# Output projection of a hybrid attention block as a Strassen product over pairs of token tiles

## Chip, cores, metric

One core of a Trainium2 chip runs the kernel. The metric is the device time of one execution in microseconds. Engines are named as in the profile: PE (TensorE), DVE (VectorE), ACT (ScalarE), POOL (GpSimd), SP (SyncE, which here only issues DMAs); PEld is PE's weight load.

## The reference

One layer over 1024 tokens of width 1024, all in float32. The lines around the change:

```python
h = rmsnorm(x, norm_mix_pre)
proj = h @ w_in                     # q, k, v, forget, conv parts, two gates
...                                 # short convolution ya, forgetting attention yb
merged = sigmoid(gate_conv) * (ya @ w_branch[0]) + sigmoid(gate_attn) * (yb @ w_branch[1])
m = merged @ w_out                  # 1024 x 1024 by 1024 x 1024
x = x + rmsnorm(m, norm_mix_post)
h = rmsnorm(x, norm_ffn_pre)
f = (silu(h @ w_gate) * (h @ w_up)) @ w_down
out = x + rmsnorm(f, norm_ffn_post)
```

The output is (1, 1024, 1024) in float32.

## The kernel before

*Precision.* Each float32 operand is split into a high part, `hi` = the value rounded to fp32r by an ACT copy, and a low part, `lo` = value minus `hi`, a DVE subtraction (`split`). A product is three matmuls: hi*hi, hi*lo, lo*hi (`mm3`). So each operand costs one ACT pass and one DVE pass, and all 128x128 by 128x512 matmuls come in threes.

*Strassen.* The projections and the FFN already use the Strassen-Winograd form on 2x2 blocks: seven products (A11 B11, A12 B21, S1 T1, S2 T2, S3 T3, S4 B22, A22 T4) instead of eight. `prod` is one product of 12 matmuls (4 blocks along K, three each) into a PSUM bank; `strassen` runs the products and combines them with DVE additions (`c12`, `c22`, `c21`; P1 = A11 B11 is kept, c11 comes out of the bank `b1`). `prep_first` and `prep_rest` load a weight pair into `raw`, make the S sums on DVE (in the one buffer `sx` and in place) and split them. A product that adds to a bank must wait until DVE has read the bank's earlier content.

*Stages, in order.* (1) v projection. (2) 18 projection jobs (`jobs`: four q/k, four `z`, two `gb`, eight gates), the operands of two jobs prepared ahead. (3) Attention, with the conv branch's products as filler. (4) `pbb`: the attention branch's product by `w_branch[1]`, for two token halves `n` and eight column blocks `d`, gated by `sg` loads and added into `um`, which is [128, 8, 1024], the merged activations with the width on the partitions. While `n` is 0, one row block of `w_out` a step is loaded and split into `woh`/`wol`. (5) `e_mm`/`e_norm`: for each of eight 128-token tiles, 2 x 8 x 3 matmuls into two `pm` banks, then the post-norm, the residual sum, the store of the new `x` to `x2_dram`, the FFN's pre-norm, eight transposes (`tp`) and two copies back into `um`. The norm of a tile runs under the matmuls of the next. (6) `f_first` for seven FFN columns: only P1 and c11, which need only the first four tiles; they are stored in `pre_dram`. The last tile's norm runs under the first four. `h2_sums` makes, for four slices, the T operands of the FFN, slice `sl` out of tiles `sl` and 4+`sl`; each uses `sx` for T1 and T2 and a `raw` for T3 and T4. (7) The FFN columns and (8) the down projection.

*Order.* A scheduler of the language places each instruction on its engine's queue by its own model; the queues run in order. The lists in `strict` fix program order for some stages (attention); stages (4) to (7) have none. Buffers are `wpool` tiles: `raw` 3, `hi` 4, `lo` 3, `sx` 1, `s4` 1, `s4h`/`s4l` 2 each.

All arithmetic goes through small helpers, so the profile gives one line, L76, to nearly every instruction (the call in `InOrder`); groups are told apart by tile names. There `c` stands for c12, c21, c22, `b` for the banks b1 to b3, `s` for s4 and others, since numbers are left out.

Of the kernel before, what the change touches and what calls it, by code (L numbers as in the profile page):

```python
# [17 lines left out]
P = 128  # L18
# [28 lines left out]
def block_kernel(  # L47
# [69 lines left out]

    def copy(o, a):
        nc.scalar.activation(o, a, AF.Copy)
# [16 lines left out]
    stat.tile([P, 24], F32, name="pad", bufs=1)  # L136
# [12 lines left out]
    ri_dram = [dpool.tile([2, S], F32, name=f"ri_dram{j}") for j in range(4)]  # L149
    sg_dram = [dpool.tile([2, P, S], F32, name=f"sg_dram{d}") for d in range(8)]  # L150
# [195 lines left out]

    def v_tile(st, ops):
# [36 lines left out]
    for st in range(ST):  # L384
# [5 lines left out]
        if st + 3 == ST:  # L390
            ax_close()
            w0, w0_close = pool("w0", side="right")
            r0 = w0.tile([P, KT, P], F32, name="r0")
            h0, l0 = (w0.tile([P, KT, P], F32R, name=n) for n in ("h0", "l0"))
# [429 lines left out]

    zts = {}
# [3 lines left out]
    for ij, (kind, j, _, _) in enumerate(jobs):  # L829
# [57 lines left out]
        else:  # L887
# [286 lines left out]
    wo_pool, wo_close = pool("wo", side="right")  # L1174
    woh = wo_pool.tile([P, KT, D], F32R, name="woh")
    wol = wo_pool.tile([P, KT, D], F32R, name="wol")
# [25 lines left out]
    ha_pool, ha_close = pool("ha")  # L1202
    hah = ha_pool.tile([P, 2, 4, NC], F32R, name="hah")
    hal = ha_pool.tile([P, 2, 4, NC], F32R, name="hal")
    fp, fp_close = pool("f", 2)
    ep, ep_close = pool("e")
    gpo = bcast_row(norm_mix_post[0], ep, name="gpo")
    gpr = bcast_row(norm_ffn_pre[0], ep, name="gpr")

    def e_mm(st):  # L1210
        ss = slice(st * P, (st + 1) * P)
        mh, ml = hi_t(), lo_t()
        split(mh, ml, um[:, :, ss])
        pm = []
        for n in range(2):
            ns = slice(n * NC, (n + 1) * NC)
            ps = psm.tile([P, NC], F32, tag="mm", name="pm")
            for k in range(KT):
                mm3(
# [11 lines left out]
    def e_norm(st, pm):  # L1231
        ss = slice(st * P, (st + 1) * P)
        xt = xts.popleft()
        if st + 1 < ST:
            xts.append(load_xt(st + 1))
# [385 lines left out]
```

## Time and profile before

| | |
|---|---|
| median of 3 runs | 1350.15 us (1349.59 to 1350.45) |
| the profiled execution | 1350.04 us |
| its span, first to last instruction | 1348.2 us |
| PE busy | 1328.5 us (99%) |
| DVE busy | 932.3 us (69%) |
| ACT busy | 535.2 us (40%) |
| POOL busy | 127.2 us (9%) |
| `pm` matmuls, first to last start | 610.9 to 704.3 us |
| bytes moved by DMA | 186.36 MB |

Matmuls are pipelined and their ends are modelled: a busy PE says that work was queued. The spacing of starts says how fast it went. Idle time is shown before an instruction, with what released it. Timeline rows with a count merge neighbours of one kind.

### The profile page before, as it was taken

Reading aid. Unit: us, or ns where it says so; the run is one execution under the profiler, and the core shown is the slowest. Engines: PE = TensorE matmul, PEld = TensorE weight load, DVE = VectorE, ACT = ScalarE, POOL = GpSimd, SP = SyncE. Lnnn points to the kernel's source line nnn. Section 1 sums busy time; section 2 is a strip of 40 time slices with the busy share of each in tenths; the row PEclk is TensorE's granted clock in tenths of the full one; section 3 lists DMA queues with packets and bytes.
Section 4 is the critical chain, followed back from the end, with each engine's and each line's share of the span. In section 5 each row is a group of like instructions: output and inputs, shape, how many; then the busy total and the mean of one; then the engine's idle time right before and its main releaser. Section 6 shows DMA issues by size and latency. Waiting matters only on the chain.

```text
span 1348.2 us, 17709 instructions
## 1 busy us (share of the span) xinstructions
PE 1328.5 (99%) x6753; PEld 1098.9 (82%) x6753; DVE 932.3 (69%) x1445; ACT 535.2 (40%) x851; POOL 127.2 (9%) x252
## 2 busy tenths in 40 slices
PE   9999999999999999999999999999999999999997
PEld 7978888888887778788887788888888888888886
DVE  6974668754556766775669698776677766677585
ACT  6642222243345756613547232223222323444452
POOL 0001000011112112000002121100111011000000
PEclk9999999999999999999999999999999999999999
DMA  5332422333325444362235565332323236965541
GB/s 189 118 109 86 126 70 71 105 123 109 102 82 192 158 142 165 126 218 79 94 110 175 170 200 167 102 100 80 117 102 118 93 111 240 361 235 196 161 164 63
DMA packets 153256, 186.36 MB, mean 138 GB/s; under 512 B 9409, under 2 KB 106753, under 8 KB 153170
## 3 DMA queue, kind: packets, MB, share of 16 engines
q1 hardware_dynamic: 138434, 136.67, 32.4%
q0 software_dynamic: 14736, 48.54, 9.3%
q8 instruction: 53, 0.87, 0.3%
q14 instruction: 33, 0.27, 0.1%
HBM read 136.10 MB, written 49.09 MB: 137 GB/s over the span
## 4 chain that ended last, share of the span: by engine, by line
PE 58%; DVE 3%; DMA 2%; issue 1%; ACT 1%; POOL 0%; DVEq 0%; SPq 0%; POOLq 0%; ACTq 0%
PE b L76 28%; PE pd L76 15%; PE pm L76 5%; PE pbb L76 3%; PE pba L76 2%; PE po L76 1%; PE tps L76 1%; PE sp L76 1%; DMA pre_dram<-s 1%; DMA tk<-in_w_down_dram 1%; DVE tt L76 0%; DVE lo L76 0%; PE tp L76 0%; DMA pre_dram<-c 0%; ACT tt L76 0%
## 5 line engine op out<-in xcount | busy, mean ns | idle before, releaser
L76 DVE TENSOR_TENSOR c<-c,b 128x512 f32<-128x512 f32 x195 | 132.9, 682 | 91.4 <-PE b L76 72.3
L76 DVE TENSOR_TENSOR lo<-raw,hi 128x1024 fp32r<-128x1024 f32 (+1 forms) x93 | 112.0, 1204 | 83.1 <-PE b L76 68.8
L76 ACT ACTIVATE hi<-raw 128x1024 fp32r<-128x1024 f32 (+1 forms) x100 | 101.7, 1018 | 127.9 <-PE b L76 75.7
L76 PE MATMUL b<-hth,hi 128*128 128x512 f32 x352 | 137.3, 390 | 0.0
L76 PE MATMUL b<-hth,lo 128*128 128x512 f32 x352 | 137.0, 389 | 0.0
L76 PE MATMUL b<-htl,hi 128*128 128x512 f32 x352 | 136.9, 389 | 0.0
L76 ACT ACTIVATE hi<-sx 128x1024 fp32r<-128x1024 f32 x41 | 43.5, 1062 | 220.9 <-PE b L76 195.3
L76 PEld LDWEIGHTS b<-hth,hi 128*128 128x128 f32 x352 | 66.1, 188 | 14.6 <-DVE c L76 1.0
L76 PEld LDWEIGHTS b<-hth,lo 128*128 128x128 f32 x352 | 66.1, 188 | 13.8
L76 PEld LDWEIGHTS b<-htl,hi 128*128 128x128 f32 x352 | 66.1, 188 | 13.7
L76 DVE TENSOR_TENSOR lo<-sx,hi 128x1024 fp32r<-128x1024 f32 x41 | 50.2, 1224 | 33.6 <-PE b L76 31.4
L76 PE MATMUL b<-hah,hi 128*128 128x512 f32 x176 | 69.0, 394 | 1.2 <-ACT c L76 1.2
L76 PE MATMUL b<-hal,hi 128*128 128x512 f32 x176 | 68.5, 389 | 0.0
L76 PE MATMUL b<-hah,lo 128*128 128x512 f32 x176 | 68.4, 390 | 0.0
L76 DVE TENSOR_TENSOR sx<-raw 128x512 f32<-128x512 f32 x78 | 53.6, 688 | 19.1 <-DMA raw<-in_w_in_dram 9.0
L76 PE MATMUL pd<-hi,lo 128*128 128x512 f32 x160 | 62.3, 389 | 0.0
L76 PE MATMUL pd<-hi 128*128 128x512 f32 x160 | 62.0, 390 | 0.0
L76 PE MATMUL pd<-ghi 128*128 128x512 f32 x148 | 57.6, 390 | 0.0
L76 PE MATMUL pd<-glo,ghi 128*128 128x512 f32 x148 | 57.6, 389 | 0.0
L76 PE MATMUL pd<-ghi,glo 128*128 128x512 f32 x148 | 57.6, 389 | 0.0
L76 PE MATMUL b<-hT34h,hi 128*128 128x512 f32 x136 | 53.0, 390 | 0.4 <-DVE c L76 0.4
L76 PE MATMUL b<-hT34h,lo 128*128 128x512 f32 x136 | 52.9, 389 | 0.0
(368 smaller groups left out, 3359.9 us busy)
## 6 DMA issues: line engine op xcount, KB each, us to landing
raw<-in_w_gate_up_dram SPq DMA_DIRECT2D x51, 512.0 KB, 3.8
raw<-in_w_in_dram SPq DMA_DIRECT2D x35, 512.0 KB, 3.8
a_dramS<-um POOLq DMA_DIRECT2D x44, 256.0 KB, 2.8
a_dramA<-um POOLq DMA_DIRECT2D x33, 256.0 KB, 2.8
xt<-in_x_dram SPq DMA_DIRECT2D x16, 512.0 KB, 4.3
sg<-sg_dram SPq DMA_DIRECT2D x32, 256.0 KB, 4.6
graw<-a_dramS SPq DMA_DIRECT2D x14, 512.0 KB, 4.0
sg_dram<-c POOLq DMA_DIRECT2D x24, 256.0 KB, 2.3
```

The lines of the kernel that those rows point to most:

```text
L76: ins = getattr(self.engine, name)(*args, **kw)
```

## The change

`w_out` gets the Strassen form too, over pairs of 128-token tiles: A is the 2x2 of `um` (two halves of the width by two tiles of a pair), B is the 2x2 of `w_out`. Four pairs of seven products of 12 matmuls take the place of eight tiles of 48.

- *Weights.* `wo_ops(n)`, called once after each of 16 projection jobs, loads four 128x128 blocks of `w_out`, makes T1 to T4 with four POOL subtractions, splits all seven operands (896 wide) and stores the two parts in a new DRAM buffer `wo_dram`, [7, 4, 128, 2, 512], from POOL. `r0`, `h0`, `l0` have one buffer each.
- *`pbb`.* The loads and splits of `w_out` go; `load_wo` loads B11, B21, T2, T1 (16 x 512 KB, split already) between the `sg` loads. The operands of pair 0 and the sums of pairs 0 and 1 start in the second half.
- *Pairs.* `first`/`second` run A11 B11 and A12 B21 for all four pairs. The kept P1 and c11 of pairs 0 to 2 take the three `raw` buffers. Then, pair by pair, `rest_ops` of the next pair, the five other products, `e_norm` of the pair before. The S sums are POOL additions in place in `um` (`gtt`).
- *Norm.* `e_norm` now takes two tiles at once. POOL multiplies three of four blocks by the gain `gpo`, DVE adds to `x` in four half rows, and both tiles' transposes (16) follow. The scaled rows go into `tt` and into the kept buffer.
- *Buffers.* The `x` tiles of the weights become the FFN's operands afterwards (B11, B21 and T1 to T4 of the activations). While `f_first` runs, its P1 lies in halves of `sx`, not in an own buffer.

```diff
+    def wo_ops(n):
+        k, c = divmod(n, 4)
+        r, h, l = w0_tiles()
+        for slot, (row, half) in enumerate(((k, 1), (k, 0), (4 + k, 0), (4 + k, 1))):
+            nc.sync.dma_start(
+                r[:, slot], wout_d[row * P : (row + 1) * P, half * NC + c * P : half * NC + (c + 1) * P]
+            )
+        for o, a, b in ((4, 0, 1), (5, 3, 4), (6, 3, 0), (7, 2, 5)):
+            gtt(r[:, o], r[:, a], r[:, b], ALU.subtract)
+        split(h[:, 1:], l[:, 1:], r[:, 1:])
+        for hl, t in enumerate((h, l)):
+            nc.gpsimd.dma_start(
+                wo_dram[:, k, :, hl, c * P : (c + 1) * P].rearrange("o p m -> p o m"), f32(t[:, 1:])
+            )
...
+        if 0 < ij < len(jobs) - 1:
+            wo_ops(ij - 1)
...
+    def load_wo(o, k):
+        nc.sync.dma_start(f32(wo[o][:, :, k, :]), wo_dram[o, k])
...
             nc.sync.dma_start(sg, sg_dram[d][1, :, ns])
+            load_wo(*loads.pop(0))
...
-            if n == 0:
-                wr = flat(raw_t())
-                nc.sync.dma_start(wr, wout_d[d * P : (d + 1) * P, :])
-                split(woh[:, d, :], wol[:, d, :], wr)
+            if n and d == 1:
+                first_ops(0, [s4h_t(), s4h_t()], [s4l_t(), s4l_t()])
...
+    def first(i):
+        b1s[i] = bank(psm, "b1")
+        prod(b1s[i], firsts[i]["A11"], both(wo[B11]), True)
+        t = raw_t() if i < 3 else ep.tile([P, KT, P], F32, name="keep")
+        keeps.append(flat(t).rearrange("p (a b) -> p a b", a=2))
+        copy(keeps[i][:, 0], b1s[i])
+    def second(i):
+        b1 = b1s.pop(i)
+        prod(b1, firsts[i]["A12"], both(wo[B21]), False)
+        mul(keeps[i][:, 1], b1, gpo[:, n1])
+        square(b1, qas[i][:, 0:1])
...
+    def e_norm(i, c12, c21, c22):
+        qa, qb = qas[i], st2("qb")
+        for c, acc in ((c12, qb[:, 0:1]), (c21, qa[:, 1:2]), (c22, qb[:, 1:2])):
+            square(c, acc)
+        for c, ns in ((c12, n2), (c21, n1), (c22, n2)):
+            gtt(c, c, gpo[:, ns], ALU.mult)
+        add(qa, qa, qb)
+        rs = scale2(qa)
...
+        rs = scale2(ssq)
+        for e in range(2):
...
+            nc.vector.scalar_tensor_tensor(
+                tt[e], xp[e], rs[:, e : e + 1], gpr, op0=ALU.mult, op1=ALU.mult
+            )
...
+    for step in (0, 1, 2, 3):
+        first(step)
+        if step:
+            second(step - 1)
+    second(PAIRS - 1)
...
-    for st in range(ST):
-        cur = e_mm(st)
+    for i in range(PAIRS):
+        nxt = rest_ops(i + 1) if i + 1 < PAIRS else None
+        _, *cur = strassen(ops, wob, psm, fe, keeps[i][:, 0])
         if prev is not None:
-            e_norm(st - 1, prev)
...
+            e_norm(i - 1, *prev)
+        if i > 1:
+            half_split(B11, i - 2)
+        prev, ops = cur, nxt
+    hb.append(both(x_tile(2)))
+    for i in range(2):
+        half_split(B21, i)
+    p1s = flat(wtile("sx", 1))
     for f in range(4):
-        f_first(f)
-    e_norm(ST - 1, prev)
+        f_first(f, p1s[:, (n1, n2)[f % 2]])
+    e_norm(PAIRS - 1, *prev)
```

The order on the engines, at three places.

POOL during the projection jobs, before, where it only issues stores (`so` and `c` are results of the q/k jobs):

```order
L76 DMA qk_dram_67<-so 128x512
L76 DMA qk_dram_68<-so 128x512
L76 DMA qk_dram_67<-c_1128 128x512
L76 DMA qk_dram_67<-c_1114 128x512
L76 MEMSET s_1296 128x8
L76 DMA qk_dram_67<-c_1039 128x512
L76 DMA qk_dram_68<-c_1249 128x512
L76 DMA qk_dram_68<-c_1235 128x512
```

And after:

```order
L76 DMA qk_dram_67<-so 128x512
L76 TENSOR_TENSOR r_1297<-r_1297 128x128 x4
L76 DMA qk_dram_68<-so 128x512
L76 DMA wo_dram<-h_1298 128x7x128
L76 DMA wo_dram<-l_1299 128x7x128
L76 TENSOR_TENSOR r_1459<-r_1459 128x128 x4
L76 DMA wo_dram<-h_1460 128x7x128
L76 DMA qk_dram_67<-c_1129 128x512
L76 DMA wo_dram<-l_1461 128x7x128
L76 DMA qk_dram_67<-c_1115 128x512
L76 DMA qk_dram_67<-c_1040 128x512
```

The four subtractions and the two stores of each `wo_ops` call stand among the stores of the first jobs; the last of the 16 calls ends among the first four stores of `ya`, that is with the seventh job, not one for each job.

DVE where the norm of a late tile ends, before (tile 5; `tt` is what the transposes read, `lo<-raw,hi` the split of an FFN weight):

```order
L76 SCALAR_TENSOR_TENSOR tt<-pm,r_6379,gpo 128x512 x2
L76 TENSOR_TENSOR xt<-xt,tt 128x1024
L76 TENSOR_SCALAR va<-ssq 128x1
L76 RECIPROCAL r_6391<-sq 128x1
L76 SCALAR_TENSOR_TENSOR t_6395<-r_6391,va 128x1
L76 TENSOR_SCALAR t_6395<-t_6395 128x1
L76 TENSOR_TENSOR r_6396<-r_6391,t_6395 128x1
L76 SCALAR_TENSOR_TENSOR tt<-xt,r_6396,gpr 128x1024
L76 TENSOR_TENSOR lo<-raw,hi 128x1024
```

And after, where the norm of pair 2 ends (its two tiles are scaled into `tt` and `raw`; `keep` and `c_6560` belong to pair 3):

```order
L76 TENSOR_TENSOR c_6560<-c_6560,b_6547 128x512
L76 TENSOR_TENSOR lo<-raw,hi 128x1024
L76 TENSOR_SCALAR va<-ssq 128x2
L76 RECIPROCAL r_6650<-sq 128x2
L76 TENSOR_TENSOR t_6654<-r_6650,va 128x2
L76 TENSOR_TENSOR keep<-keep,b_6546 128x512
L76 TENSOR_TENSOR t_6654<-t_6654,r_6650 128x2
L76 TENSOR_TENSOR lo<-raw,hi 128x1024
L76 TENSOR_SCALAR t_6654<-t_6654 128x2
L76 TENSOR_TENSOR r_6655<-r_6650,t_6654 128x2
L76 SCALAR_TENSOR_TENSOR tt<-xt,r_6655,gpr 128x1024
L76 SCALAR_TENSOR_TENSOR raw<-xt,r_6655,gpr 128x1024
```

The split of the weight came behind the scaled rows and now two such splits come ahead of them, with the last sum of the next pair between; on PE the 16 transposes of the pair stand directly behind the 60 matmuls of the next pair.

DVE ahead of the first FFN product, before (`htl` and `hcl` are T and B22 operands of the activations, `sx` and `raw` their sums; the `sgf` row is the FFN's first gate):

```order
L76 SCALAR_TENSOR_TENSOR tt<-xt,r_6694,gpr 128x1024
L76 TENSOR_TENSOR htl<-sx,hth 128x8x128
L76 TENSOR_TENSOR htl<-raw,hth 128x8x128
L76 TENSOR_TENSOR lo<-raw,hi 128x1024
L76 TENSOR_TENSOR sx<-um 128x512
L76 TENSOR_TENSOR raw<-um 128x512
L76 TENSOR_TENSOR hcl<-um,hch 128x4x128 x3
L76 TENSOR_TENSOR sx<-um,sx 128x512
```

And after (`x_6923`, `x_6924`, `x_6925` and `x_6926` are T1, T2, T3 and T4):

```order
L76 SCALAR_TENSOR_TENSOR keep<-xt,r_6882,gpr 128x1024
L76 TENSOR_TENSOR lo<-raw,hi 128x1024
L76 TENSOR_TENSOR raw<-um 128x512
L76 TENSOR_TENSOR sgf<-sgf,c_7104 128x512
L76 TENSOR_TENSOR x_6925<-raw,x_6925 128x4x128
L76 TENSOR_TENSOR lo<-raw,hi 128x1024
L76 TENSOR_TENSOR sx<-um 128x512
L76 TENSOR_TENSOR sx<-um,sx 128x512
L76 TENSOR_TENSOR raw<-um,sx 128x512
L76 TENSOR_TENSOR x_6923<-sx,x_6923 128x4x128
L76 TENSOR_TENSOR x_6924<-sx,x_6924 128x4x128
```

Before, three slices' `sx` sums stand ahead of the last tile's scaled row, and one slice behind it. Now all four slices' `sx` sums stand behind the last pair's.

More of the change, by code (lines that the diff above doesn't have):

```diff
@@ new lines, in block_kernel, with st2, scale2, square @@
+    xts = deque([load_xt(0), load_xt(1)])
+    gpr = bcast_row(norm_ffn_pre[0], ep, name="gpr")
+    def st2(name, bufs=2):
+        return ep.tile([P, 2], F32, tag=name, name=name, bufs=bufs)
+    def scale2(ssq):
+        return rms_scale(ssq, None, lambda n, w: st2(n), 2)
+    def square(src, acc):
+        junk = ep.tile([P, NC], F32, tag="junk", name="junk")
+        nc.scalar.activation(junk, src, AF.Square, accum_out=acc)
+    for i in range(1, PAIRS):
+        first_ops(i, hi_t(), lo_t())
+        if i > 1:
+            sums_31(i, s4_t() if i == 2 else ep.tile([P, 4, P], F32, name="s3"))
+        sums_24(i)
```

191 lines of the change are left out of this document (118 added, 73 removed).

## Prediction

> **What bounds the kernel now.** I read the page's busy line first, then the table of stretches, then the `pm` tile, then the chain of waits. In the stretch rows the columns are: stretch, its length, busy PE, PEld, DVE, ACT, POOL, granted clock, DMA share, GB/s.
>
> ```profile
> PE 1328.5 (99%) x6753; PEld 1098.9 (82%) x6753; DVE 932.3 (69%) x1445; ACT 535.2 (40%) x851; POOL 127.2 (9%) x252
> 200.00:300.00 100.00, 100.00 (x443) 82.81 (x442) 70.12 (x100) 27.53 (x34) 7.03 (x13) 1.00 0.35 105
> 566.00:611.00 45.00, 45.00 (x201) 37.24 (x200) 34.94 (x48) 14.26 (x18) 0.00 (x0) 1.00 0.56 176
> 632.00:706.00 74.00, 73.65 (x351) 60.62 (x350) 49.30 (x109) 33.82 (x77) 3.21 (x6) 1.00 0.29 100
> 706.00:744.00 38.00, 36.84 (x163) 29.09 (x162) 34.54 (x51) 27.55 (x43) 7.58 (x14) 1.00 0.52 173
> L76 PE MATMUL pm<-woh,hi x128: 389/389/481, 610.9 to 703.8; 128*128 128x512 f32 x128
> 693.80 10.89 PE pm L76 x48
> 704.69 0.87 PE tp L76 x8
> ```
>
> TensorE is the limit everywhere. Around `w_out` (611 to 706 us) it waits for almost nothing (0.35 us in 74), and in 706 to 744, where the FFN is entered, DVE is nearly as full as PE (34.5 of 38 us). So a matmul removed is worth its issue time, 10.89/48 = 0.227 us, not the 0.389 us of its row; and DVE has little left to give in just the stretch that is rewritten. The profiled execution took 1350.04 us (span 1348.2), 0.1 under the median of 1350.15; the sum is against 1350.0.
>
> **The change, part by part.** The durations used:
>
> ```profile
> 731.98 1.89 DVE L76 TENSOR_TENSOR hcl<-um,hch 128x512 fp32r<-128x512 f32 x3
> 726.40 1.22 DVE L76 TENSOR_TENSOR htl<-sx,hth 128x1024 fp32r<-128x1024 f32 x1
> 727.53 1.22 DVE L76 TENSOR_TENSOR htl<-raw,hth 128x1024 fp32r<-128x1024 f32 x1
> 714.33 1.40 DVE L76 SCALAR_TENSOR_TENSOR tt<-pm,r,gpo 128x512 f32<-128x512 f32 x2
> 725.20 1.28 DVE L76 SCALAR_TENSOR_TENSOR tt<-xt,r,gpr 128x1024 f32<-128x1024 f32 x1
> 654.28 0.15 DVE L76 TENSOR_SCALAR va<-ssq 128x1 f32<-128x1 f32 x1 [1.22 <-ACT tt L76]
> 655.54 1.29 DVE L76 SCALAR_TENSOR_TENSOR tt<-xt,r,gpr 128x1024 f32<-128x1024 f32 x1
> 656.75 1.06 ACT L76 ACTIVATE hi<-um 128x1024 fp32r<-128x1024 f32 x1 [2.08 <-PE pm L76]
> 646.60 0.61 ACT L76 ACTIVATE tt<-pm 128x512 f32<-128x512 f32 x1
> 647.08 0.21 ACT L76 ACTIVATION_READ_ACCUMULATOR tt<-pm 128x1 f32 x1
> L76 POOL DMA_DIRECT2D sg_dram<-c x24 | 13.0, 543 | 59.2 <-ACT c L76 55.4 <-DVE c L76 3.8
> L76 POOL DMA_DIRECT2D c_dram<-cT x1 | 0.5, 549 | 0.1
> L76 POOL TENSOR_TENSOR cb<-cb,mask x64: 452/459/471, 393.7 to 541.5; 128x128 f32<-128x128 f32 x64
> L76 SPq DMA_DIRECT2D cb<-c_dram x10: 339/382/434, 156.2 to 518.0; - x10
> raw<-in_w_in_dram SPq DMA_DIRECT2D x35, 512.0 KB, 3.8
> pre_dram<-s POOLq DMA_DIRECT2D x7, 256.0 KB, 3.4
> ```
>
> Back to back on DVE, a 512-wide operation costs 0.60 us (three end after 1.89), a 1024-wide one 1.13 (start to start), a two-scalar one 0.70 (half of 1.40) or 1.28; from `va` to the scaled rows of a norm 1.26 us pass (654.28 to 655.54).
>
> 1. *Matmuls.* 8 tiles x 2 halves x 8 x 3 = 384 become 4 pairs x 7 products x 4 x 3 = 336; the 64 transposes stay. 48 x 0.227 = **-10.9 us**, all on the path.
>
> 2. *Projections.* Each of 16 `wo_ops` adds four loads on SP, four POOL subtractions, one 896-wide copy on ACT (7/8 of 1.06 = 0.93), one 896-wide split on DVE (7/8 of 1.13 = 1.0) and two POOL stores. The order puts all 16 DVE splits between the first job's S2 sum and the seventh job's last: 44 products of 12 matmuls, 120 us of PE, 8.0 us for each of 15 steps. DVE (70 of 100 us) and ACT have room for 1 us in 8. With one buffer, a step is: four issues (1.5), landing (at most the 3.8 of a load eight times as large), the last subtraction 0.46, 0.93, 1.0: 7.7 us, inside 8.0. A projection load behind them on SP is two jobs (38 us) ahead of its use; a split that waits on DVE holds the sums behind it, and the S3 product waits for S2's sum. A store has 896 pieces of 512 B. 64 such pieces (`c_dram`) took 0.549 us and 128 of 2 KB 0.543, so the count does not show; the other end is 7 x 0.543 = 3.8. I take the near end: **0**, range 0 to +36 (rival B); work added off the path cannot gain.
>
>    The Trainium skill, "DMA: Bandwidth & Descriptors", Anatomy of one DMA, says that many descriptors can be emitted before their cost shows; by that the store stays near 0.54 and the term at 0, and the two rows agree as far as 128 pieces go.
>
> 3. *The `pbb` stage.* Eight `w_out` loads with their splits go; 16 loads of 512 KB come, alternating with the `sg` loads on SP: 12.6 MB in 45 us, 280 GB/s against 176 at a DMA share of 0.56, by proportion 0.89. It fits; a late `sg` is covered by eight PSUM banks of 2.7 us each. 0, at worst one load, +3.8. A gain is excluded, PE being full there. The 12 later loads (6.3 MB in the 27 us until T3 is needed) are no denser: 0.
>
> 4. *First half of the pair stage.* Eight half-products, 21.8 us, need only copies (0.61) and splits made one or two products earlier: 0, or up to +2 for the copy that the second half-product waits for.
>
> 5. *Transposes between pairs.* The order puts 16 transposes of pair i-1 directly behind pair i's five products (60 matmuls, 13.6 us), and SP, POOL, ACT and DVE must finish that pair's norm by then. From the last product of pair 0, DVE's rows up to the first scaled tile are: its own last sum 0.8, five sums 3.0, four half rows 2.8, splits 1.1 + 3 x 0.6, 1.28, two norm tails (1.26, and 1.9 with the totals), and about 1 us waiting for ACT's squares (0.61 + 0.21 each). That is 15.0 against 13.6: PE waits 1.5. Pair 1 the same: 1.5. For pair 2 six 1024-wide splits are in the row (three of weights, three of `um`), 6.8 instead of 2.9, and its own sum ends 3.0 late because DVE queues: 3.0 + 3.0 + 2.8 + 6.8 + 1.3 + 3.2 + 1.0 = 21.1, against 3.4 (transposes with their wait) + 13.6 = 17.0 on PE: 4.1. Pair 3 has 19 us of `f_first` as cover: 0. Sum +7.1; before, this stage lost 0.3. **+6.8**, ends 0 (everything hidden, as now) and +14 (POOL serial, below). POOL's three products a pair lie between 0.46 and 4 x 0.46 = 1.84 each; even 5.5 us ends before the half row that reads the last, so 0.
>
> 6. *Entry to the FFN.* Now three of four slices of `h2_sums` are done before the last transposes; the last slice runs from 730.77, and its FFN operands end at 744.1, when PE gets there:
>
> ```profile
> 729.40 1.04 PE L76 MATMUL tp<-ident,tt 128*128 128x128 f32 x8
> 730.77 0.69 DVE L76 TENSOR_TENSOR sx<-um 128x512 f32<-128x512 f32 x1
> 742.88 1.22 DVE L76 TENSOR_TENSOR lo<-raw,hi 128x1024 fp32r<-128x1024 f32 x1
> 726.54 0.50 PE L76 MATMUL b<-hah,hi 128*128 128x512 f32 x1 [1.16 <-ACT c L76]
> 756.68 0.47 PE L76 MATMUL b<-hch,s4h 128*128 128x512 f32 x1 [1.46 <-DVE c L76]
> 771.64 0.47 PE L76 MATMUL b<-hch,s4h 128*128 128x512 f32 x1 [0.67 <-DVE c L76]
> ```
>
>    Afterwards `sx`, which every slice needs for T1 and T2, holds the P1 of `f_first`, so no slice can make T1 or T2 before f_first(3)'s P1 has been copied (0.6), issued (0.54) and stored (3.4): 4.6 us after that product. Then 36 sums and splits of 512 and two of 1024 stand on DVE before the first FFN product's operands: 21.6 + 2.3, ending at 28.5. PE has 84 matmuls and 16 transposes: 19.1 + 1.7 = 20.8. Gap 7.7. The old slice's 12.1 us (730.77 to 742.88) held 12 rows of 0.60 and three of 1.13, 10.6: 14% more, for waits on ACT. I take half of that on the 23.9, a gap of 9.4; the 1.16 us now lost at 726.54 falls into it: **+8.2**, ends 0 (DVE has it ready, as now) and +11 (the whole 14%, the 1.16 staying).
>
> 7. *After the entry.* The operands then stand before PE needs them, so the two waits at 756.68 and 771.64 go: **-2.1**, ends -2.1 and 0.
>
> Sum: -10.9 + 6.8 + 8.2 - 2.1 = +2.0, and 1350.0 + 2.0 = **1352 us**. About 0.2% (2.7 us) is what a measurement of this kernel can tell from no change.
>
> **Rivals.**
>
> *A, faster: the norm keeps up.* If the scheduler's order fits, the waits of step 5 vanish: 1350.0 - 10.9 - 0.3 - 2.1 + 8.2 = 1345, and with the entry hidden too 1337. For it: PE lost 0.3 us in this stage before. Against it: a norm had one tile per 10.9 us and now has two per 13.6, with 18 us of DVE rows in the worst window. It decides where the norm of pair 2 ends within 17 us.
>
> *B, slower: the weight stores bind POOL.* A step is 4 x 0.46 + 0.93 + 2 stores; it passes 8.0 us when a store takes over 2.6. At 3.8 it costs 15 x (10.4 - 8.0) = +36, 1388; at 3.0, +12. Only the missing row for 896 pieces speaks for it.
>
> *C, slower: POOL and DVE hold each other up.* DVE would stand still while POOL multiplies: three of about 1.5 us (between the ends above) in each of three windows, +13, 1365. Against it, DVE operations that read two tensors in SBUF beside the POOL additions of attention are no longer than elsewhere:
>
> ```profile
> L76 DVE TENSOR_TENSOR yb<-yb,rb 128x512 f32<-128x512 f32 x7 | 4.8, 684 | 0.0
> ```
>
>    The Trainium skill, "GPSIMD Engine Reference", Key points, speaks for it: GpSimd shares its SBUF interfaces with VectorE and contends with DVE instructions that have two SBUF inputs. By that rule 1365, by the row 1352; POOL is seldom busy in that stage, so the row is weak.
>
> **How the numbers follow.** The forecast, waits that return the saving, 1346 to 1357: 0.50 (0.05 of it under 1347.3, 0.25 within 0.2%, 0.20 above). A: 0.22. B: 0.13. C: 0.10. Some other late load: 0.05, slower. Faster 0.27, same 0.25, slower 0.48. Range 1342 to 1368: leaves out A with the entry hidden (about 0.08) and B with stores above 3.3 us (about 0.11).
>
> **What would show it.** Right: 336 product matmuls at 0.227 us; PE waits of 1 to 2, 1 to 2 and about 4 us at `tp`, released by DVE `tt`/`raw`; one wait of 6 to 11 us at the first product of the FFN, released by DVE `lo`; none at 756 and 771; projections at 100% PE; `wo_dram` stores near 0.54 us. Wrong: a store over 2.6 us with PE waiting on DVE sums before 250 us; DVE operations longer beside POOL; transposes that find `tt` ready.

## The result and the profile after

The changed kernel takes 1460.08 us (median of 4 runs, 1458.55 to 1461.75) against 1350.28 us before: ratio 1.0814, 95% interval 1.0796 to 1.0833. It is 110 us slower. The prediction was 1352 us, range 1342 to 1368.

The first and second part of the changed kernel's profile page; the second gives busy TensorE and its granted clock in 40 slices, in tenths.

```profile
PE 1348.7 (93%) x6705; PEld 1108.2 (76%) x6705; DVE 962.5 (66%) x1450; ACT 549.0 (38%) x871; POOL 236.5 (16%) x376
PE   9985756889999999999997879999999999999998
PEclk9998778999999999999999989999999999999999
```

The 48 matmuls are gone (6753 became 6705), and yet TensorE is busy 20 us longer and idle 88 us longer. Both lie in two places: slices 3 to 9 (73 to 328 us, the projection jobs) and 22 to 24 (765 to 874 us, the pair stage and the entry to the FFN). The clock falls below nine tenths within these slices and nowhere else. Stretches of the two kernels (stretch, its length, busy PE, PEld, DVE, ACT, POOL, granted clock, DMA share, GB/s), the first of before, the rest of after:

```profile
60.00:407.10 347.10, 344.66 (x1549) 285.22 (x1548) 212.10 (x299) 109.05 (x137) 31.35 (x59) 1.00 0.33 102
...
60.00:498.90 438.90, 369.04 (x1547) 298.81 (x1545) 228.10 (x314) 120.21 (x152) 96.26 (x155) 0.91 0.42 123
659.20:702.70 43.50, 43.50 (x193) 36.04 (x192) 28.67 (x40) 5.79 (x9) 10.60 (x7) 1.00 0.78 275
702.70:858.00 155.30, 132.00 (x577) 105.46 (x576) 113.38 (x176) 80.66 (x145) 47.76 (x47) 0.94 0.49 166
858.00:1237.70 379.70, 379.70 (x1673) 314.25 (x1672) 286.20 (x400) 109.79 (x140) 44.44 (x82) 1.00 0.37 119
```

The first two rows run from 60 us to the first attention product. The same matmuls take 438.9 us instead of 347.1, 91.8 more: 67.4 of it TensorE standing (69.9 against 2.4) and 24.4 of it TensorE busy for longer. The granted clock accounts for 22.3 of the 24.4: it was 0.50 for 44.5 us of these matmuls. From the first `pbb` product to the first of the down projection before 563.7 us passed (567.43 to 1131.09) and now 578.6 (659.21 to 1237.78), 14.9 more, and 1.9 are added behind that: 91.8 + 14.9 + 1.9 = 108.6, the difference of the spans.

A step of the weight combinations, on POOL (start, duration, engine, what, and in brackets the idle time before it):

```profile
229.56 0.96 POOL L76 DMA_DIRECT2D wo_dram<-l  x1 [6.10 <-issue]
230.53 1.82 POOL L76 TENSOR_TENSOR r<-r 128x128 f32<-128x128 f32 x4
234.75 0.94 POOL L76 DMA_DIRECT2D wo_dram<-h  x1 [2.40 <-ACT hi L76]
240.20 0.94 POOL L76 DMA_DIRECT2D wo_dram<-l  x1 [4.50 <-DVE zt L76]
245.40 0.94 POOL L76 DMA_DIRECT2D wo_dram<-h  x1 [1.39 <-ACT h L76]
```

A store is issued in 0.95 us, but the next POOL store starts 4.7 to 7.1 us after it started (5.4 in the median), whatever the profile names as its releaser ("issue" in 13 of the 32 cases); a subtraction may follow at once. What it waits for is the landing of the store before it: the stores that start at 229.56, 234.75 and 240.20 landed at 234.44, 239.89 and 244.60, and the next of POOL's stores started 0.31, 0.31 and 0.80 us later (in the third case ACT's copy ended last). With two such stores a step cannot be shorter than some 11 us, and the 16 stores of `h` start from 86.49 to 293.34, 13.8 us a step, against the 8.0 that TensorE leaves. Who pays, on DVE and on TensorE:

```profile
234.52 1.09 DVE L76 TENSOR_TENSOR l<-r,h 128x896 fp32r<-128x896 f32 x1 [9.06 <-DMA wo_dram<-l]
236.67 0.68 DVE L76 TENSOR_TENSOR c<-c,b 128x512 f32<-128x512 f32 x1
237.40 0.79 PE L76 MATMUL b<-hT34h,hi 128*128 128x512 f32 x1 [9.74 <-DVE c L76]
```

DVE stands 9 us at the split of the step, until the store of the step's one buffer `l` has landed; the job's sum stands behind it in order, and the S3 product behind the sum.

The second place, TensorE's waits from the pair stage to the FFN:

```profile
752.79 1.09 PE L76 MATMUL tp<-ident,tt 128*128 128x128 f32 x8 [0.55 <-DVE tt L76]
755.09 1.06 PE L76 MATMUL tp<-ident,raw 128*128 128x128 f32 x8 [1.21 <-DVE raw L76]
773.05 1.06 PE L76 MATMUL tp<-ident,raw 128*128 128x128 f32 x8 [1.21 <-DVE raw L76]
794.97 1.97 PE L76 MATMUL tp<-ident,tt 128*128 128x128 f32 x8 [7.19 <-DVE tt L76]
796.74 1.66 PE L76 MATMUL tp<-ident,raw 128*128 128x128 f32 x8
816.98 0.73 PE L76 MATMUL b<-x,hi 128*128 128x512 f32 x2 [1.97 <-ACT sx L76]
851.92 1.22 PE L76 MATMUL b<-x,hi 128*128 128x512 f32 x2 [5.73 <-ACT hi L76]
855.36 0.80 PE L76 MATMUL b<-x,lo 128*128 128x512 f32 x1 [2.22 <-DVE lo L76]
827.86 0.69 DVE L76 TENSOR_TENSOR sx<-um 128x512 f32<-128x512 f32 x1 [5.38 <-DMA pre_dram<-sx]
```

The transposes behind the wait of 7.19 us take 1.97 and 1.66 us where others take 1.06: the granted clock was 0.50 from 791.2 to 798.0 us. In the last row DVE stands for 5.38 us at the first sum of `h2_sums`, until the store of P1 out of `sx` has landed; the T operands of the FFN stand behind it. And a thing that no row of before shows, DVE beside POOL's products (two windows, DVE and then POOL):

```profile
751.45 1.28 DVE L76 SCALAR_TENSOR_TENSOR tt<-xt,r,gpr 128x1024 f32<-128x1024 f32 x1
752.65 2.29 DVE L76 SCALAR_TENSOR_TENSOR raw<-xt,r,gpr 128x1024 f32<-128x1024 f32 x1
791.15 1.23 DVE L76 TENSOR_SCALAR t<-t 128x2 f32<-128x2 f32 x1
792.42 1.18 DVE L76 TENSOR_TENSOR r<-r,t 128x2 f32<-128x2 f32 x1
...
751.57 2.29 POOL L76 TENSOR_TENSOR c<-c,gpo 128x512 f32<-128x512 f32 x1 [3.17 <-ACT junk L76]
790.92 1.44 POOL L76 TENSOR_TENSOR keep<-keep,gpo 128x512 f32<-128x512 f32 x1 [1.51 <-ACT junk L76]
792.32 1.26 POOL L76 TENSOR_TENSOR c<-c,gpo 128x512 f32<-128x512 f32 x1
```

The two scaled rows are the same operation and take 1.28 and 2.29 us; POOL's product beside them takes 2.29 instead of 1.26. Taking the normal lengths off the ends, they take turns: POOL's work begins when the first row ends (about 752.6), the second row's when POOL ends (about 753.7). A row of two elements per partition, 0.16 us elsewhere, lasts 1.2.

### The profile page after: what moved, and what is told of

Read it like the earlier page. It is cut to its first block, busy times and chain, and to the rows that moved or that the text cites. A ratio compares the mean times of both kernels' runs of the same rounds, so it can differ in the third digit from the quotient of the medians.

```text
span 1456.8 us, 18048 instructions
## 1 busy us (share of the span) xinstructions
PE 1348.7 (93%) x6705; PEld 1108.2 (76%) x6705; DVE 962.5 (66%) x1450; ACT 549.0 (38%) x871; POOL 236.5 (16%) x376
## 4 chain that ended last, share of the span: by engine, by line
PE 52%; DVE 3%; issue 2%; DMA 1%; ACT 1%; POOL 0%; DVEq 0%; SPq 0%; POOLq 0%; ACTq 0%
PE b L76 29%; PE pd L76 14%; PE pbb L76 3%; PE pba L76 2%; PE po L76 1%; PE tps L76 1%; PE sp L76 1%; DMA tk<-in_w_down_dram 1%; DVE c L76 0%; DVE raw L76 0%; DVE t L76 0%; DVE lo L76 0%; DMA pre_dram<-sx 0%; DVE x L76 0%; DVE xt L76 0%
## 5 line engine op out<-in xcount | busy, mean ns | idle before, releaser
L76 PE MATMUL b<-x,hi 128*128 128x512 f32 x1232 | 384.3, 393 | 10.7 <-ACT hi L76 5.7
L76 PEld LDWEIGHTS b<-x,hi 128*128 128x128 f32 x1232 | 231.9, 189 | 61.7 <-ACT hi L76 6.1
L76 PE MATMUL b<-x,lo 128*128 128x512 f32 x616 | 241.5, 392 | 2.4 <-DVE lo L76 2.4
L76 PEld LDWEIGHTS b<-x,lo 128*128 128x128 f32 x616 | 116.6, 189 | 28.0 <-DVE lo L76 3.5
L76 ACT ACTIVATE hi<-sx 128x1024 fp32r<-128x1024 f32 (+1 forms) x43 | 44.7, 1039 | 209.8 <-PE b L76 170.5
L76 DVE TENSOR_TENSOR l<-r,h 128x896 fp32r<-128x896 f32 (+1 forms) x17 | 18.7, 1098 | 79.9 <-ACT h L76 44.7
L76 DVE TENSOR_TENSOR lo<-sx,hi 128x1024 fp32r<-128x1024 f32 (+1 forms) x43 | 51.5, 1198 | 24.3 <-PE b L76 23.6
L76 PEld LDWEIGHTS b<-hT34h,hi 128*128 128x128 f32 x136 | 27.8, 204 | 42.5 <-DVE c L76 36.6
L76 PE MATMUL b<-hT12h,lo 128*128 128x512 f32 x136 | 54.1, 398 | 4.5 <-DVE lo L76 4.5
L76 PE MATMUL b<-hT34l,hi 128*128 128x512 f32 x136 | 56.3, 414 | 0.0
```

What stands on the lines that cost most here:

```text
L76: ins = getattr(self.engine, name)(*args, **kw)
```

## The experiments

Landmarks of each kernel's trace: the start of the attention (first score product), the time from the first `pbb` product to the first of the down projection, and the median.

| kernel | attention starts | pbb to down | median us |
|---|---|---|---|
| before | 407.1 | 563.7 | 1350.3 |
| the change | 498.9 | 578.6 | 1460.1 |
| one_per_job | 429.4 | 579.9 | 1392.1 |
| long_pieces | 441.8 | 578.1 | 1401.5 |
| one_per_job_long | 409.1 | 578.2 | 1368.2 |
| split_stores (one run) | 415.6 | 579.3 | 1376.0 |
| stores_on_sp (one run) | 411.5 | 580.9 | 1373.4 |
| four_steps | 407.8 | 580.9 | 1366.7 |
| no_pool_products | 428.2 | 571.7 | 1382.5 |
| products_on_dve | 409.2 | 579.3 | 1367.8 |
| p1_elsewhere | 409.1 | 565.3 | 1354.7 |
| kept_busy (one run) | 409.6 | 580.8 | 1371.5 |
| late_splits | 409.2 | 565.5 | 1355.2 |
| products_later | 408.9 | 573.5 | 1363.8 |
| late_no_products | 408.7 | 559.1 | 1348.3 |
| products_later_3 | 409.1 | 564.1 | 1353.9 |
| products_later_3_early_splits | 408.6 | 565.3 | 1356.6 |

### The projections

**one_per_job.** The step is kept in program order on every engine:

```diff
         if 0 < ij < len(jobs) - 1:
+            strict[0] = engines
             wo_ops(ij - 1)
+            strict[0] = ()
```

> Only the order changes: each of the 16 weight-combination steps is kept in its own projection job (one per 19 us of TensorE) instead of 16 within seven jobs. Theory 1 (POOL is the bound of a step: each of its two 896-piece stores holds back the next POOL store for about 5 us, so a step takes 13.8 us where 8 us were left): 13.8 fits into 19, all of the 91.8 us lost before the attention comes back, and the time is 1460 - 92 = 1368 us, within 1364 to 1374, with the projections' granted clock at 1.00. Rival A (the work of a step itself, its loads on SP and its split on DVE, holds the sums wherever it stands): a step's waits stay, at least a third of the loss with them, 1395 us or more.

Measured: 1392.08 us, ratio 1.0308 (1.0293 to 1.0324). 69.5 of the 91.8 us came back, 22.3 stayed, a quarter, where theory 1 left nothing and the rival at least a third. Neither was right as it stood: the crowding is most of it, but a hold is left.

**long_pieces.** The layout in DRAM is turned so that a partition's seven blocks are one piece:

```diff
-    wo_dram = dpool.tile([7, 4, P, 2, NC], F32, name="wo_dram")
+    wo_dram = dpool.tile([4, 2, 4, P, 7, P], F32, name="wo_dram")
...
-                wo_dram[:, k, :, hl, c * P : (c + 1) * P].rearrange("o p m -> p o m"), f32(t[:, 1:])
+                wo_dram[k, hl, c], f32(t[:, 1:])
...
```

> The stores stay crammed into seven jobs and move the same bytes, but the DRAM layout makes each store 128 pieces of 3.5 KB instead of 896 of 512 B (the later loads then read pieces of 512 B, in two DMAs each). Theory 1, in the form that the number of pieces holds POOL: the next POOL store follows within 1 us, a step falls to the 8 to 10 us of its own chain, and at most a quarter of the 91.8 us stays: 1368 to 1392 us. Rival B (448 KB through POOL's queue take 5 us whatever the pieces): the gap after a store stays near 5 us and the time near 1460 us, 1445 or more.

Measured: 1401.47 us, ratio 1.0379 (1.0363 to 1.0394); 34.7 of the 91.8 us stay, more than the quarter that was allowed. The pieces are what holds POOL, as its rows show; bytes are the same:

```profile
94.80 0.56 POOL L76 DMA_DIRECT2D wo_dram<-h  x1 [1.39 <-ACT h L76]
95.40 0.55 POOL L76 DMA_DIRECT2D qk_dram<-c  x1
96.00 0.54 POOL L76 DMA_DIRECT2D wo_dram<-l  x1
```

What stays is the step's own chain: the 16 stores of `h` start from 84.92 to 241.37, 10.4 us a step, still over 8.0.

**one_per_job_long.** Both edits together.

> One combination step per projection job and stores of 128 pieces of 3.5 KB, both together. In the kernel with one step per job POOL still stood for 4 to 5 us behind each weight store, the subtractions of the next step started that much later, and ACT's copies stood behind the step's copy: 22.3 us of the projections stayed lost. Theory 1 (the pieces hold POOL, and nothing else in a step is too long for 19 us): the first attention product starts at 407 to 411 us instead of 429.4, and the time is 1392 - 20 = 1372 us, within 1369 to 1375. Rival A (a step's own rows hold ACT and DVE wherever the step stands): at least half of the 22.3 us stays, 1380 us or more.

Measured: 1368.24 us, ratio 1.0135 (1.0118 to 1.0152); the attention starts at 409.1, as theory 1 had it; the time is 0.8 under its range. The four cases make a square: of 91.8 us, long pieces alone leave 34.7, one step per job alone 22.3, both 2.0. The rest of one_per_job was POOL's hold, not the step's rows.

**split_stores.** As one_per_job, each store issued as two:

```diff
-            nc.gpsimd.dma_start(
-                wo_dram[:, k, :, hl, c * P : (c + 1) * P].rearrange("o p m -> p o m"), f32(t[:, 1:])
+            for o in (slice(0, 4), slice(4, 7)):
+                nc.gpsimd.dma_start(
+                    wo_dram[o, k, :, hl, c * P : (c + 1) * P].rearrange("o p m -> p o m"),
+                    f32(t[:, 1 + o.start : 1 + o.stop]),
...
```

> As the kernel with one step per job (pieces of 512 B), with each weight store issued as two, of 512 and of 384 pieces. It asks what the hold of 4 to 5 us behind a store of 896 pieces goes by. Theory 1a (a rate: the pieces of a store must be taken up before the next store starts, 896 in about 5 us): after 512 pieces the next POOL store starts about 2.8 us later, after 384 about 2.1, and the time stays near 1392 us. Rival L (a threshold between 128 and 896 pieces above which POOL stands): after the smaller ones the next store follows within 1 us, and the time is near 1370 us.

Measured: 1376.00 us in one run. POOL's rows in one step (512 pieces, 384 pieces, then a store of 128):

```profile
349.61 0.77 POOL L76 DMA_DIRECT2D wo_dram<-h  x1 [0.88 <-ACT h L76]
350.78 0.76 POOL L76 DMA_DIRECT2D wo_dram<-h  x1 [0.40 <-issue]
355.66 0.58 POOL L76 DMA_DIRECT2D sg_dram<-c  x1 [4.12 <-issue]
```

The 384 follow the 512 after 0.40 us, so no rate per store holds there; the store behind them, which would make 1,024 under way, waits 4.12 us: the 512 landed at 355.35, and it starts 0.31 us later. That fits a bound on the pieces under way, issued and not yet landed, and the landing times of all 17 traces bear it out. Among their 3,531 DMAs from POOL's queue none was issued with more than 960 pieces under way, its own among them (896 and 64, in one_per_job at 159.69). 220 would have brought the sum to 1,024 or more, had they followed at once. All of them waited: 164 started 0.30 to 0.39 us after the landing that brought the sum down to 960 or less, the others later, and none earlier. It is pieces and not bytes: 704 KB under way, the last store's among them, were too many here, while long_pieces had up to 1,408 KB under way in fewer pieces.

**stores_on_sp.** As one_per_job, with `nc.sync.dma_start` for the two stores.

> As the kernel with one step per job (896 pieces of 512 B per store), with the weight stores issued by SP instead of GpSimd. It asks whose the hold behind a store of 896 pieces is. Theory 1b (POOL's queue alone holds back its next store): SP issues each store in 1 to 2 us and goes on, the first attention product starts at 408 to 412 us and the time is near 1368 us. Rival M (any queue that issues 896 pieces stands for about 5 us): SP's loads behind the stores come late, the attention starts at 415 us or later and the time is 1374 us or more.

Measured: 1373.44 us in one run; the attention starts at 411.5. The stores' durations on SP (minimum, median, maximum in ns):

```profile
L76 SPq DMA_DIRECT2D wo_dram<-h x16: 366/377/378, 110.0 to 400.6; - x16
```

The same 896 pieces take SP 0.37 us, and the next DMA of its queue started within 0.71 us of the store's start in 24 of 32 cases; two such stores were under way at once, 1,792 pieces. The hold is POOL's queue's own. The time is 5 us above the 1368 of theory 1b and just under the 1374 of its rival: 2.7 us of that lie between `pbb` and the down projection (580.9 against 578.2 in one_per_job_long), and one run does not say why.

**four_steps.** Four of the 16 calls, in jobs 4, 8, 12 and 15; the loads read `wo_dram[o, 0]` for every `k`.

> Only 4 of the 16 combination steps are done, each in a job of its own, and the later loads read the four that there are (their values repeat), so the rest of the kernel is as in the change. It isolates the pair stage and the entry to the FFN. Theory 1 (everything before the attention is the steps' doing, and the stages behind cost +14.9 us as in the traces): the projections end where they did before the change, and 1350.2 + 14.9 + 1.9 for the end of the kernel give 1367 us, 1364 to 1370. If it comes out clearly under 1364, the stages behind suffer from what the projections left late; if over 1372, the steps were not the cause.

Measured: 1366.68 us, ratio 1.0118 (1.0101 to 1.0135), as expected; the attention starts at 407.8. So the two losses add up, to within some 2 us: the stretch from `pbb` to the down projection took 580.9 us here, in an execution of 1368.61 us, against 578.6 in the changed kernel.

### The pair stage and the entry to the FFN

**no_pool_products.** As one_per_job, without the loop of `gtt(c, c, gpo[:, ns], ALU.mult)`.

> As the kernel with one step per job, and in the norm the twelve GpSimd products by the post-norm weights are left out (the values are unscaled), with the order on all other engines unchanged. Theory C (a GpSimd product and a DVE operation that needs the same access to SBUF take turns, so that a DVE operation of 0.16 us lasts 1.2 and one of 1.28 lasts 2.3): the long rows go (1.0 each, some 2 per pair and 3 for pair 2), DVE rows of the norm fall back to 0.16 and 1.28, and the waits at the transposes shrink by 5 to 7 us, so 1361 to 1363 if the kernel with one step per job has 1368. Rival D (the waits are DVE's own rows, as predicted, and GpSimd's part is hidden): the same time as one step per job, within 1.5 us.

Measured: 1382.51 us, ratio 1.0246 (1.0221 to 1.0271), 9.6 us under one_per_job, of which 8.2 lie between `pbb` and the down projection. With the same order on DVE, the rows are short and one wait is left, 3.61 us:

```profile
715.33 0.16 DVE L76 TENSOR_SCALAR t<-t 128x2 f32<-128x2 f32 x1
715.73 1.28 DVE L76 SCALAR_TENSOR_TENSOR tt<-xt,r,gpr 128x1024 f32<-128x1024 f32 x1
...
717.07 1.22 PE L76 MATMUL tp<-ident,tt 128*128 128x128 f32 x8 [3.61 <-DVE tt L76]
```

The waits at transposes go from 0.53 + 1.22 + 1.21 + 7.22 to 3.61, 6.6 us less, inside theory C's 5 to 7. The 8.2 us hold 1.7 more, because fewer matmuls ran at the granted clock of 0.50 (10.3 us instead of 13.6).

**products_on_dve.** As one_per_job_long, with `mul(c, c, gpo[:, ns])` in that loop.

> As the kernel with one step per job and long pieces, with the twelve products of the norm on DVE instead of GpSimd. Theory C (GpSimd and DVE take turns, 8.2 us of this stage): the 8.2 us come back, and 1.8 us of DVE rows per pair go back in ahead of the half rows, of which pair 2 pays all and pairs 0 and 1 up to 1.5 each: 3 to 6 us faster than one step per job with long pieces. Rival D (DVE's own rows are what PE waits for, GpSimd's part is hidden): 2 to 5 us slower.

Measured: 1367.76 us, 0.5 under one_per_job_long. Neither theory had that: the waits at the transposes are now 5.19 (pair 0), 0 and 5.65 us, 10.8 in all against 10.2. What the turns had cost, the rows cost.

**p1_elsewhere.** As one_per_job_long, with P1 in result buffers of the pair stage:

```diff
-    p1s = flat(wtile("sx", 1))
     for f in range(4):
-        f_first(f, p1s[:, (n1, n2)[f % 2]])
+        f_first(f, t_(fe, ("c12", "c22")[f % 2]))
```

> As the kernel with one step per job and long pieces, but the first products of the early FFN halves are copied into result buffers of the pair stage that are free by then, not into the halves of sx, so that the operand sums of slices 0 and 1 need not wait for the stores of these products. Theory E (step 6 of the prediction: sx holds the sums back): slices 0 and 1 are made before the last transposes, the waits at the first FFN products (5.7 and 2.8 us) and at the early halves (2.8 us) go, and it is 6 to 11 us faster than one step per job with long pieces. Rival F (the last pair's norm and DVE's rows after the last transposes set the entry): at most 2 us faster.

Measured: 1354.73 us, ratio to before 1.0037 (1.0021 to 1.0052), 13.5 us under one_per_job_long. The waits of 5.7 and 2.8 us at the first FFN products are gone, and so is the slow stretch behind them; the early halves (the products of `f_first`) wait for 1.97 us in all. The `sx` sums of slices 0 and 1 now start at 707.08 and 715.92 us, ahead of the last transposes (728.48); in one_per_job_long the first started at 736.38. Theory E holds, with more than it expected.

**kept_busy.** As one_per_job_long, with `for _ in range(48): nc.tensor.transpose(tp[:, 0, :], ident, ident)` ahead of pair 2's first transposes.

> As the kernel with one step per job and long pieces, with 48 more transposes of the identity (some 5.5 us of TensorE, overwritten by the real ones) in the 7.2 us wait ahead of pair 2's transposes. Theory G (a long wait is paid again in a lower granted clock after it): the two rows of eight transposes behind the wait, 1.97 and 1.66 us in the changed kernel, fall to about 1.06, the wait row itself shrinks to 1 to 2 us, and the stage is 1.5 to 2 us shorter. Rival H (the slow rows come from the transposes' operands or their PSUM buffers): they stay, and the stage is as long or longer.

Measured: 1371.53 us in one run, 3.3 over one_per_job_long. The rows behave as theory G says:

```profile
698.41 5.40 PE L76 MATMUL tp<-ident 128*128 128x128 f32 x48
705.81 1.09 PE L76 MATMUL tp<-ident,tt 128*128 128x128 f32 x8 [2.00 <-DVE tt L76]
707.10 1.06 PE L76 MATMUL tp<-ident,raw 128*128 128x128 f32 x8 [0.20 <-DVE qa L76]
```

The same transposes take 1.09 and 1.06 us instead of 1.97 and 1.92. The stage did not get shorter: the early halves behind waited longer (2.07, 0.89 and 3.10 us). The scheduler also placed 29 rows of ACT and 16 of DVE differently, so the total says nothing on the theory, and the 1.5 to 2 us are not shown.

**late_splits.** As p1_elsewhere:

```diff
-hb.append(both(x_tile(2)))
+hb.append(both(x_tile(5, wy)))
...
-    hb += [both(x_tile(n, p)) for n, p in ((0, wx), (3, wx), (4, wy), (5, wy))]
+    hb += [both(x_tile(n, p)) for n, p in ((0, wx), (2, wx), (3, wx), (4, wy))]
```

> As the kernel with the first products elsewhere, with the B21 operands of the FFN kept in the buffer of T4's weights instead of T2's, which comes free one product row later (behind the last product of pair 3): their two splits, 2.4 us of DVE ahead of the norm of pair 2, move behind that norm. Theory I (DVE's rows in the window of pair 2 set its wait, as step 5 of the prediction has it, with the half splits among them, which it left out): the wait of 7.2 us falls to 3 to 5 and the time from 1354.7 to 1350 to 1352.5 us. Rival J (the turns with GpSimd set it, whatever stands on DVE): the wait stays over 6 us and the time over 1353.5.

Measured: 1355.22 us, ratio 1.0041 (1.0027 to 1.0055), no faster. Its longest waits:

```profile
702.35 1.09 PE L76 MATMUL tp<-ident,tt 128*128 128x128 f32 x8 [3.43 <-DVE tt L76]
728.76 0.73 PE L76 MATMUL b<-x,hi 128*128 128x512 f32 x2 [1.56 <-ACT c L76]
760.51 0.47 PE L76 MATMUL b<-hch,s4h 128*128 128x512 f32 x1 [1.73 <-DVE c L76]
778.39 0.74 PE L76 MATMUL b<-x,hi 128*128 128x512 f32 x2 [1.30 <-DVE c L76]
```

Theory I had the wait right (7.21 to 3.43 us) and the time wrong: behind it TensorE waits 5.98 us where p1_elsewhere waits 2.85. Of the 3.8 us, 3.1 were given back within 80 us, and 1.2 more went to a stretch at half clock that p1_elsewhere does not have (3.41 us from 665.81).

**products_later.** As late_splits, with `((c21, n1), (c12, n2), (c22, n2))` in the products' loop, kept in order on GpSimd.

> As the kernel with late splits, with GpSimd's three products of a pair in the order c21, c12, c22 instead of c12, c21, c22, so that none is ready before the pair's last sum and none meets the scaled rows of the pair before; all else in the same order. Theory C (DVE and GpSimd take turns): the second scaled row of pairs 0 and 1 falls from 2.30 to 1.28 us and the small rows of pair 2's norm from 0.9 to 1.2 to 0.16, the waits of 1.2 us at the second transposes go to 0.4 or less, and it is 2 to 5 us faster than late splits: 1346 to 1349. Rival K (the half rows now wait for the later products): the waits at the first transposes grow by 1 to 2 us each, and it is no faster.

Measured: 1363.79 us, ratio 1.0108 (1.0093 to 1.0123), 8.6 slower than late_splits. The second scaled rows are 1.28 us and the waits of 1.2 us are gone, as expected, but one wait is new:

```profile
738.92 1.94 PE L76 MATMUL tp<-ident,tt 128*128 128x128 f32 x8 [11.68 <-DVE tt L76]
...
706.63 0.54 POOL L76 DMA_DIRECT2D pre_dram<-c  x1 [10.74 <-ACT sq L76]
728.89 1.27 POOL L76 TENSOR_TENSOR keep<-keep,gpo 128x512 f32<-128x512 f32 x1
```

The second POOL row is the first of pair 3's products. It now stands behind the eight stores of the early halves on POOL's queue, which start at 706.63, and pair 3's norm stands behind it; in late_splits the same product started at 706.90. That is neither C nor K; it is a queue that was not looked at.

**late_no_products.** late_splits without the products.

> As the kernel with late splits, with GpSimd's twelve products of the norm left out (values unscaled). It bounds what the order of the products can bring: by theory C all of the waits at the transposes but 1 to 2 us go and it comes to 1344 to 1347 us; if GpSimd's part is no longer on the path, it is within 1.5 us of late splits.

Measured: 1348.33 us, ratio 0.9986 (0.9977 to 0.9995), 6.9 under late_splits; a little above the 1344 to 1347 of theory C. This is what the kernel would take if the products cost nothing.

**products_later_3** and **products_later_3_early_splits.** The new order for `i < PAIRS - 1` only; the second on p1_elsewhere instead of late_splits.

> As the kernel with late splits, with the products in the order c21, c12, c22 for pairs 0 to 2 only; pair 3 keeps the old order, so that its products stand ahead of the early stores on GpSimd's queue. Theory C with the cause of the loss in the kernel with later products named (pair 3's products came behind the stores there, and its transposes waited 11.7 us): the second scaled rows stay at 1.28 us, the waits of 1.2 us at the second transposes stay away, pair 3 waits for nothing, and the time is 1350 to 1354 us, 1 to 5 below late splits. Rival K (the half rows wait for the later products): no better than late splits, 1355 or more.

> As the kernel with the first products elsewhere (splits as there), with the later products for pairs 0 to 2. If late splits only moved the wait (3.8 us less at pair 2's transposes came back as 3.9 us more behind the entry), the two are alike with later products as well: 1350 to 1354 us, within 1.5 us of the kernel with late splits and later products. If the late splits are worth their wait once the products are out of the way, this one is 2 to 4 us slower than that.

Measured: 1353.87 us, ratio 1.0024 (1.0015 to 1.0034), and 1356.64 us, 1.0045 (1.0030 to 1.0060). The wait of 11.7 us is gone, so its cause is shown. The gain over late_splits is 1.4 us, at the edge of what was expected and not clear of noise, as the two intervals overlap: with the second rows short, sums wait for turns instead (0.48, 0.65 and 0.66 us), and pair 2's wait is 4.01. The second kernel is 2.8 us slower, as its second case asked. But of the 2.2 us between the two traces only 1.2 lie between `pbb` and the down projection; a stretch at half clock in the down projection (3.41 us from 1143.05), which the first kernel does not have, makes 1.7. So the late splits are worth some 1 us here, and the rest is the clock. No version with the whole computation beat before; products_later_3 is the best, 3.6 us behind.

## Why the prediction was wrong, step by step

**Step 1, right.** 48 matmuls are gone.

**Step 2, the step that failed.** Taken at 0, range 0 to +36; measured +91.8. The sum priced a store by its issue row: the near end, 0.54 us, or 3.8. The issue is 0.95 us, inside the bounds, and the price was not in it: POOL's next store waits until the store of 896 pieces has landed, and starts 3.7 to 6.1 us after its issue ended. No row of before could show that: its stores have 128 pieces or fewer, and at most 768 were under way at once. Two further terms were mis-sized. The step's own chain was put at 7.7 us and is 10.4 without the hold (long_pieces: 34.7 us lost with no hold at all). The sum had one subtraction of 0.46 us behind the loads; in that trace 3.2 us pass in the mean from the start of the first of the four subtractions to the end of the last, single ones lasting up to 1.4 us, and DVE comes to the split 1.0 us late, being at the job's rows. And lost time was counted as waits alone, while some 22 of the 91.8 us are what matmuls lost at a granted clock of 0.50 behind the waits. Whether second buffers for `h0` and `l0` would have kept DVE going was not tried.

The Trainium skill, "DMA: Bandwidth & Descriptors", Anatomy of one DMA, says that many descriptors can be emitted before their cost shows: true here up to 960 pieces under way, not for 1,024, and the measurement decides.

**Step 3, right.** 43.5 us, all busy, at 275 GB/s where 280 was expected.

**Step 4, right.** No wait was expected in the first half of the pair stage, and none came.

**Step 5, close in size and wrong in cause.** +7.1 expected in waits of 1.5, 1.5 and 4.1; measured 1.76, 1.21 and 7.19, in all 10.2. Without POOL's products 3.6 are left (no_pool_products), so 6.6 go with the turns. How much of pair 2's wait of 7.2 belongs to which is not shown, though: without the products it is 3.6, with two splits moved instead 3.4 (late_splits), and with both 3.1 (late_no_products), so either step alone halves it and the second brings little. POOL's products were costed at 0, by their own length; what they do to DVE was rival C, given 0.10.

**Step 6, right in cause, too small.** One wait of 9.4 us at the first FFN product was expected; 5.73 + 2.22 came. `sx` was the cause: taking P1 out of it gave 13.5 us back against the +8.2. The difference is waits at the early halves, which were not in the sum (1.97 and 1.23 us are the longest), and two stretches at half clock, from 818.48 and from 849.20.

**Step 7, right.** No wait from 858 to 1237.7 us.

**The pair stage in sum**: -10.9 of matmuls, +19.6 of idle time (23.3 in the stretch to 858 us, 3.7 before), and 5.9 of slow clock (11.75 us of matmuls at a granted clock of 0.50) make +14.6 of the measured +14.9. Of the +1.9 behind it, 1.35 is a wait of TensorE for ACT's `hi` at 1244.73, in the down projection, which before does not have; why it comes is open.

**The rivals.** B named the place, the engine and who waits, and asked for a store over 2.6 us: its condition was met by the hold, not by the issue, and its 1388 us was 72 too low. C was real, 8.2 us instead of 13. The row it was weighed against was no evidence at all: none of the eight `yb<-yb,rb` rows of before overlaps a product of POOL (the nearest ends 0.43 us ahead of one). The DVE rows that do run beside them there read a bank of PSUM or a few numbers a partition, and a row that reads PSUM is not held up (last section). A did not come: even with the projections mended, 18 us remained.

## What to carry to other kernels

Price a store by what the next one on its queue does, not by its own row: a GpSimd store of many short pieces was issued in 1 us and held its queue for 5, until it had landed. Room in time alone took 69.5 of the 91.8 us away and longer pieces alone 57.1; room with longer pieces took 89.8, and room with SP 87.4 (one run). An elementwise operation that is moved to GpSimd "for free" is paid by the DVE row it meets, and by whatever stands behind it on GpSimd's queue. A wait removed from TensorE can come back behind it when the engine that caused it has no room there: late_splits took 3.8 us away and got nothing.

## What was not expected of the hardware

**The hold.** In these traces POOL's queue never had more than 960 pieces under way: a store that would bring them to 1,024 or more waits for a landing and starts 0.30 us or more after it. Stores of 128 pieces follow each other within 0.06 us, 64 followed 896 at once, and 128 behind 896 waited 4 us. Where the bound lies between 960 and 1,024 no run here shows. SP's queue had 1,792 pieces under way (0.37 us a store).

**Turns.** A GpSimd product of two SBUF tensors and a DVE row that reads two SBUF tensors do not overlap: 1.28 us becomes 2.29, and `r<-r,t`, 0.16 us elsewhere, becomes 1.18. TENSOR_SCALAR rows such as `t<-t` are held up too. Not every DVE row is: in the changed kernel `c<-c,b`, with one input in PSUM, took 673 to 683 ns in five places beside such products and 673 to 689 elsewhere, and the reciprocal at 788.29 took 0.17 us inside a product that lasted its normal 1.26. The Trainium skill, "SBUF — State Buffer", Who interferes with whom, says that DVE in a 2-port mode or with two SBUF inputs and a GpSimd operation that reads SBUF shut each other out, and that the one that comes second is blocked in full until the first ends. The trace agrees to 0.2 us, for tiny rows as for long ones (`t<-t`, 128x2, 1.23 us at 791.15): what counts is not the row's size but how much of the product is left.

**The clock.** Behind waits of 3 to 10 us, matmuls ran at a granted clock of 0.50 for 2.9 to 5.8 us, 10 times in the projections. Behind single waits of 1.77 and 2.32 us there was none, but behind one of 1.97 us there was (3.41 us from 818.48). The length of the wait alone does not decide. Within each trace the clock changes only on a grid of 3.41 us, and what counts is the idle time inside one window of the grid (columns as in the stretches above, busy TensorE first):

```profile
303.07:306.48 3.41, 2.22 (x10) 1.47 (x8) 3.41 (x6) 1.69 (x2) 0.93 (x1) 1.00 0.00 0
306.48:309.89 3.41, 2.29 (x10) 1.93 (x11) 2.80 (x4) 0.00 (x0) 1.17 (x3) 1.00 0.40 135
815.07:818.48 3.41, 1.50 (x7) 1.24 (x8) 1.39 (x2) 2.37 (x4) 1.43 (x3) 1.00 0.21 85
818.48:821.89 3.41, 3.41 (x10) 2.53 (x9) 0.63 (x1) 0.59 (x1) 0.03 (x1) 0.50 0.43 145
```

The wait of 2.32 us falls into two windows, 1.19 and 1.12 us idle, and the clock stays; the wait of 1.97 leaves 1.91 us idle in one, and the next window runs at half clock. Over the 17 traces, the ends of the kernels left out, the clock fell 55 times from 1.00, always behind a window with 1.63 us idle or more, and it stayed behind none with more than 1.94: the limit is near half a window. So whether a wait of about 2 us is paid again is luck of where it falls. The Trainium skill, "TensorE: Matmul & The Clock Gate", Part 1, gives an idle window of about 3.4 us, free-running, before the clock halves; the window's length agrees, but here half of it idle was enough, and the measurement decides.
